# Half-rank sums behind gate blocks, whole transposes of keys and betas, and a score eviction split over two engines

## The chip, the core and the metric

The program runs on one core of a Trainium2 chip. The core has five engines that each take their instructions in a fixed order, written into the program when it is built: TensorE (PE in the profile, with its weight loads as PEld), VectorE (DVE), ScalarE (ACT), GpSimd (POOL) and SyncE (SP). Engines wait for each other by semaphores; an instruction that waits holds up everything behind it on its engine. DMAs are issued from the queues of SP, ACT and POOL. The metric is the device time of one execution in microseconds, the median of several runs.

## The reference

One block of a streaming encoder over 512 frames of width 1024, all in float32. What matters here is the RWKV-7 branch with 8 heads of 64:

```python
proj = h @ w_in + b_in                      # 4864 columns, 38 blocks of 128
r, k, v, pw, pa, pg = split(p + (token_shift(p) - p) * mu)
decay, a, g = ...                           # from pw, pa, pg by small matrices
kk = normalise(k * k_k); k = k * (1.0 + (a - 1.0) * k_a)
# per frame: S = S diag(w) + (S a) b^T + v k^T ; y = S r, with a = -kk, b = kk * a
y = group_norm(rwkv7_recurrence(r, decay, k, v, -kk, kk * a)) * lnx_g + lnx_b
bonus = sum(r * k * r_k, per head) * v
y_a = ((y + bonus) * g) @ w_branch_a
...
merged = sigmoid(gate_a) * y_a + sigmoid(gate_b) * y_b   # gates: 16 of the 38 blocks
x = x + merged @ w_mix_out                  # then cross-attention and a ConvFFN
```

## The kernel before

Feature channels lie on the 128 partitions and the 512 frames along the free axis. Every large product is made of three fp32r matmuls on splits into a high and a low part (`mm3`, L159 to L163). Weights stream in units of 128x1024: SP loads a raw unit (L102, four buffers), ACT casts the high part (L114), DVE subtracts for the low part (L115). One unit feeds one of the 38 blocks of the input projection, `inproj` (L516), 24 matmuls of 128x512 each. The order of the blocks is `IN_ORDER`: 14 RWKV blocks, then 16 gate blocks (22 to 37), then the 8 blocks of the other branch. Below, "block 20" is the block that uses `win_h20`.

Work on the heads runs in pairs, j = 0 to 3. `prep` and `prep2` make the scaled sequences: `AK` (alphas and receptances) and `KBt` (betas and keys, interleaved by chunk of 64 frames; the two heads of a pair are offset by one column block, which is why it has 2·NC+1 of them). `scores` multiplies them chunk by chunk on PE (L605, 128 matmuls) and DVE evicts each of the four groups of a pair with a mask in two instructions of 64x512 (`BZ` at L609, `AK` at L610). `bonus` then takes r·k·r_k (L586), sums it per head with a matrix of ones in two matmuls (`bo`, L156 and L157, after a split by ACT at L154 and DVE at L155), multiplies by v (L589), adds a bias (L590) and stores to `dBo` (L591), to be loaded again by the group norm much later.

The 64 small triangular systems (8 chunks by 8 heads) of the recurrence are solved next. `scores` sends the alpha parts to DRAM (`dM`, L612), SP gathers them transposed into `Nm` (L654, two DMAs), and DVE runs 31 dependent steps on `Zt` (`zz`, L660 and L661; `Zt` is set by L655 first). `Zt` returns through `dZt` and `dZ` to `ZA` (L665 to L677); PE completes the inverses with 32x32 matmuls (`zh` L687, `zo` L695). A sequential loop over 8 chunks follows (L753 to L804). For each chunk it needs rows of values (`rows_v`, L734) and of keys and betas (`rows_kb`): eight transposes from 64 partitions (L746) into two PSUM tiles and two ACT copies of 128x256 (L747). All the while, blocks of the input projection fill PE. POOL issues DMAs that sum later weights in DRAM; each waits for a chosen matmul.

A scheduler orders each engine's instructions by program order and priority when the program is built. The solve, the DMAs of the solve and the chunk loop have high priority; the first three gate blocks (`NEARLY`) are written before pair 3, the others after the chunk loop, where they fill.

Of the kernel before, what the change touches and what calls it, by code (L numbers as in the profile page):

```python
# [53 lines left out]
def hybrid_block_kernel(ctx: ExitStack, tc: tile.TileContext, xT_d, mT_d, pv_d, cst_d, win_d, wk_d, wv_d,  # L54
# [15 lines left out]
    def mm_ps(name):  # L70
        return pmm.tile([P, T], F32, tag="mm", name=name)
# [435 lines left out]
    for i in range(2):  # L507
        with tc.issue_after(wdma[-1].ins):
            nc.sync.dma_start(lraw[i], lup_d[i])
    uin = Units(win_d, "win")  # L510


    NSUM = {12: 1, 13: 1, 4: 1, 5: 1, 0: 1, 1: 1, 8: 1, 9: 1, 6: 2, 7: 2, 2: 2, 3: 2, 10: 2, 11: 2,
            22: 2, 23: 1, 27: 1, 28: 1, 29: 1, 15: 4, 16: 4, 17: 4, 18: 4, 19: 4, 20: 3, 21: 2}

    def inproj(i):  # L516
        ps = mm_ps(f"in_ps{i}")
        dense(ps, uin, lambda kb: (h2[:, 0, kb, :], h2[:, 1, kb, :]), KB, NSUM.get(i, 0))
        return ps
# [41 lines left out]
    def prep2(j, pk, pr, at, Pi, Pp):  # L561
# [13 lines left out]
        V.tensor_tensor(kk, kk, at, ALU.mult)  # L575
        V.tensor_tensor(KBt[:, j, 1::2, :], c3(kk), c3(Pi), ALU.mult)
        S.activation(at, at, AF.Identity, scale=par("k_a", j), bias=oka[:, j:j + 1])
        V.tensor_tensor(pk, pk, at, ALU.mult)
        V.tensor_tensor(KBt[0:HD, j, 2::2, :], c3(pk)[0:HD], c3(Pi)[0:HD], ALU.mult)
        V.tensor_tensor(KBt[HD:P, j, 0:2 * NC:2, :], c3(pk)[HD:P], c3(Pi)[HD:P], ALU.mult)  # L580
        for e in range(2):
            hs = half[e]
            V.tensor_tensor(AK[hs, e, jc, HD:P], c3(pr)[hs], Pp[hs, :, 1:], ALU.mult)

    def bonus(j, pk, pr):
        V.scalar_tensor_tensor(pr, pr, par("r_k", j), pk, ALU.mult, ALU.mult)  # L586
        ps = rw_ps(f"bo{j}")
        sum_exact(ps, bonesr, pr, tp, "xb", f"bo{j}")
        V.tensor_tensor(pr, ps, vT[:, j, :], ALU.mult)  # L589
        S.activation(pr, pr, AF.Identity, bias=par("lnx_b", j))  # L590
        nc.scalar.dma_start(dBo[j], pr)  # L591

    def kb_cols(j, e, c):
        return KBt[half[e], j, 2 * c + 1 - e:2 * c + 3 - e, :].rearrange("p a t -> p (a t)")

    def scores(j):
        for e in range(2):
            hs, oh = half[e], half[1 - e]  # L600
            for cg in range(2):
                ps = rw_ps(f"sc{j}_{e}_{cg}")
                i0 = j * NC + cg * 4
                for i in range(4):
                    PE.matmul(ps[:, i * P:(i + 1) * P], kb_cols(j, e, cg * 4 + i), AK[hs, e, i0 + i, :],  # L605
                              start=True, stop=True)
                p3 = ps.rearrange("p (c t) -> p c t", t=P)
                m3 = scmask.unsqueeze(1).to_broadcast([P, 4, P])
                V.tensor_tensor(BZ[hs, i0:i0 + 4, :], p3[hs], m3[hs], ALU.mult)  # L609
                V.tensor_tensor(AK[oh, e, i0:i0 + 4, :], p3[oh], m3[oh], ALU.mult)  # L610
# [10 lines left out]
    for jp in range(2):  # L621
# [10 lines left out]
        for j in js:  # L632
            if j == 3:
                for i in IN_REST[:NEARLY]:
                    gate_block(i - 22)
            at, L, Pp = prep(j)
            prep2(j, pks[j], prs[j], at, L, Pp)
            scores(j)
            bonus(j, pks[j], prs[j])

    pp_ctx.close()
    pq_ctx = ExitStack()
    pq = pq_ctx.enter_context(tc.tile_pool(name="pq", bufs=1, reuse_waits="tile"))
    YB = pq.tile([P, 4, T], F32, name="YB")

# [95 lines left out]
    def rows_kb(c):  # L741
        KBr = ch.tile([P, 2, NPAIR, HD], F32, tag="KBr", name=f"KBr{c}", bufs=2)
        for e in range(2):
            ps = ch_ps(f"kbr{c}_{e}", ("kv", "s")[e])
            for j in range(NPAIR):
                PE.transpose(ps[:, j * HD:(j + 1) * HD], kb_cols(j, e, c), ident[half[e], half[e]])  # L746
            S.copy(KBr[:, e], j3(ps[:, 0:256]))  # L747
        return KBr
# [4 lines left out]
    def chunk(c, UV, KBr, SP):  # L753
# [664 lines left out]
```

## Time and profile before

| | us |
|---|---|
| median of 3 runs | 912.09 (909.4, 912.09, 913.08) |
| the profiled execution, its own time | 909.73 |
| its span in the trace | 908.0 |
| TensorE busy | 890.5 |
| VectorE busy | 687.4 |
| ScalarE busy | 510.4 |
| GpSimd busy | 129.3 |

The profile comes from one execution. A row of its timeline has the start in us from the span's start, the length, the engine, the line, the operation, output and inputs, and in brackets how long the engine sat idle before it and what ended that. A PE matmul's record begins when it enters and ends when its result is out, so records overlap: the time that a matmul takes from PE is the distance from its start to the next one's start. The granted TensorE clock was 0.998 of full speed over the run.

### The profile page before, as it was taken

What the parts mean: (1) busy time and instruction counts of PE and PEld (TensorE: products, weight loads), DVE (VectorE), ACT (ScalarE), POOL (GpSimd) and SP (SyncE); (2) the same over time, 40 slices, a digit from 0 to 9 for tenths busy, and PEclk for the clock granted to TensorE, in tenths of its full rate; (3) what the DMA queues carried; (4) which work ended last, traced back from release to release, by engine and by line L of the source; (5) the groups of instructions that cost most, each with busy time, mean ns of one, the idle gap of its engine ahead of it and who ended that gap; (6) DMA issues with size and microseconds to landing.
All of it is one profiled execution on the core that took longest, in us unless ns stands there. A gap on an engine that the chain in (4) does not pass through costs nothing. (4 is left out here: it accounts for less than half of the span.)

```text
span 908.0 us, 15914 instructions
## 1 busy us (share of the span) xinstructions
PE 890.5 (98%) x6218; PEld 776.1 (85%) x6218; DVE 687.4 (76%) x1096; ACT 510.4 (56%) x779; POOL 129.3 (14%) x159
## 2 busy tenths in 40 slices
PE   7999999999999999999999999999999999999996
PEld 6988877788877777887887778999999999999996
DVE  7884598776957585776565568788998888999674
ACT  6674675542236675234454446765665556767663
POOL 0102222010011212001112211111111111201100
PEclk9999999999999999999999999999999999999999
DMA  8878899667499749858788868898989998998963
GB/s 276 277 263 230 186 237 208 179 165 206 139 205 246 167 106 194 258 180 223 210 243 190 177 152 185 240 273 247 280 249 290 258 316 251 248 277 222 269 197 93
DMA packets 102411, 200.07 MB, mean 220 GB/s; under 512 B 25344, under 2 KB 36736, under 8 KB 102272
## 3 DMA queue, kind: packets, MB, share of 16 engines
q1 hardware_dynamic: 69504, 119.75, 41.0%
q0 software_dynamic: 25504, 67.38, 36.8%
q10 hardware_dynamic: 7328, 11.92, 3.9%
q8 instruction: 49, 0.80, 0.3%
q14 instruction: 26, 0.21, 0.1%
HBM read 187.75 MB, written 77.59 MB: 292 GB/s over the span
## 5 line engine op out<-in xcount | busy, mean ns | idle before, releaser
L126 ACT CAST wfi_h<-wfi_r 128x1024 fp32r<-128x1024 f32 x77 | 81.0, 1052 | 76.8 <-PE fx_ps L161 21.1
L160 PE MATMUL in_ps<-hT,win_h 128*128 128x512 f32 x304 | 121.9, 402 | 0.8 <-DVE pr L525 0.7
L162 PE MATMUL in_ps<-hT,win_l 128*128 128x512 f32 x304 | 120.8, 398 | 0.0
L161 PE MATMUL in_ps<-hT,win_h 128*128 128x512 f32 x304 | 120.6, 398 | 0.0
L127 DVE TENSOR_TENSOR wfi_l<-wfi_r,wfi_h 128x1024 fp32r<-128x1024 f32 x77 | 94.0, 1221 | 23.5 <-ACT wfi_h L126 23.3
L425 POOL DMA_DIRECT2D dS<-in_wfi x66 | 66.5, 1044 | 267.0 <-PE in_ps L160 132.4
L114 ACT CAST win_h<-win_r 128x1024 fp32r<-128x1024 f32 x38 | 39.8, 1048 | 71.9 <-PE in_ps L161 70.9
L115 DVE TENSOR_TENSOR win_l<-win_r,win_h 128x1024 fp32r<-128x1024 f32 x38 | 46.4, 1221 | 32.6 <-ACT win_h L114 32.5
L160 PEld LDWEIGHTS in_ps<-hT,win_h 128*128 128x128 f32 x304 | 57.0, 187 | 15.6 <-DVE pr L525 1.1
L161 PEld LDWEIGHTS in_ps<-hT,win_h 128*128 128x128 f32 x304 | 57.0, 188 | 14.0 <-issue 0.7
L162 PEld LDWEIGHTS in_ps<-hT,win_l 128*128 128x128 f32 x304 | 57.0, 187 | 13.9 <-issue 0.2
L461 POOL DMA_DIRECT2D dOs<-in_wfo x54 | 39.9, 804 | 186.0 <-PE fx_ps L160 50.9
L1245 DVE TENSOR_TENSOR wfo_l<-wfo_r,wfo_h 128x1024 fp32r<-128x1024 f32 (+1 forms) x39 | 47.2, 1210 | 13.6 <-ACT wfo_h L1244 13.5
L1244 ACT CAST wfo_h<-wfo_r 128x1024 fp32r<-128x1024 f32 (+1 forms) x39 | 40.4, 1038 | 28.2 <-PE oyz_ps L161 9.8
L161 PE MATMUL fx_ps<-hr,wfi_h 128*128 128x256 f32 x176 | 49.7, 282 | 0.0
L162 PE MATMUL fx_ps<-hr,wfi_l 128*128 128x256 f32 x176 | 49.7, 282 | 0.0
L160 PE MATMUL ox_ps<-go,wfo_h 128*128 128x256 f32 x176 | 49.6, 282 | 0.1
L160 PE MATMUL fyz_ps<-hq,wfi_h 128*128 128x256 f32 x176 | 49.3, 280 | 0.4 <-ACT p L1173 0.4
L160 PE MATMUL fx_ps<-hq,wfi_h 128*128 128x256 f32 x176 | 49.5, 281 | 0.0
L160 PE MATMUL fx_ps<-hr,wfi_h 128*128 128x256 f32 x176 | 49.4, 281 | 0.0
L162 PE MATMUL ox_ps<-go,wfo_l 128*128 128x256 f32 x176 | 49.3, 280 | 0.0
L161 PE MATMUL ox_ps<-go,wfo_h 128*128 128x256 f32 x176 | 49.3, 280 | 0.0
(418 smaller groups left out, 2727.8 us busy)
## 6 DMA issues: line engine op xcount, KB each, us to landing
dS<-in_wfi POOLq DMA_DIRECT2D x66, 512.0 KB, 8.4
wfi_r<-dS SPq DMA_DIRECT2D x44, 512.0 KB, 6.9
win_r<-in_win SPq DMA_DIRECT2D x38, 512.0 KB, 5.0
wfi_r<-in_wfi SPq DMA_DIRECT2D x33, 512.0 KB, 5.6
dS<-dS POOLq DMA_DIRECT2D x22, 512.0 KB, 5.7
dOs<-in_wfo POOLq DMA_DIRECT2D x12, 512.0 KB, 7.8
wv_r<-in_wv SPq DMA_DIRECT2D x8, 512.0 KB, 4.9
dG<-gs ACTq DMA_DIRECT2D x16, 256.0 KB, 2.6
```

The lines of the kernel that those rows point to most:

```text
L114: S.copy(hi[:, o:o + n], raw[:, o:o + n])
L115: V.tensor_tensor(lo[:, o:o + n], raw[:, o:o + n], hi[:, o:o + n].bitcast(F32), ALU.subtract)
L126: S.copy(hi, raw)
L127: V.tensor_tensor(lo, raw, hi.bitcast(F32), ALU.subtract)
L160: first = PE.matmul(ps, lh, rh, start=start, stop=False, **kw)
L161: PE.matmul(ps, lh, rl, start=False, stop=False, **kw)
L162: PE.matmul(ps, ll, rh, start=False, stop=stop, **kw)
L425: return lambda: nc.gpsimd.dma_start(s(out), src, **kw)
L461: yield lambda k=k, w=w, src=src: nc.gpsimd.dma_start(dO[n, m][:, k * P:(k + w) * P], src, **kw)
L1244: S.copy(hi[:, :n], raw[:, :n])
L1245: V.tensor_tensor(lo[:, :n], raw[:, :n], hi[:, :n].bitcast(F32), ALU.subtract)
```

## The change

Four things are changed.

First, `bonus` is cut in two. After `scores(j)`, `bonus_terms(j)` makes only the product r·k·r_k and stores it to `dBo` (128x512, from ACT's queue). After the last pair, all four are loaded back (`bt`, from ACT's queue, two buffers), split by ACT (`bhi`, which lives where `YB` comes later) and DVE (`blo`). Five gate blocks (25 to 29, up to `NMID`) are now written ahead of the solve, and the two `bo` matmuls of a pair, the product with v (`bs`), the bias and the second store to `dBo` are placed behind such a block's last matmul in program order.

Second, `KBt` loses its extra column. `prep2` writes it with four DVE instructions on 64 partitions instead of one on 128 and two on 64.

Third, `rows_kb` uses four transposes from all 128 partitions into one PSUM tile and one ACT copy of 128x512, in place of eight transposes, two tiles and two copies.

Fourth, in `scores` DVE multiplies only the right half of the `BZ` part by the mask (64x4x64); the left, alpha half is copied by ACT without a mask. Most of that half is later overwritten with the completed inverses; the one 32x32 corner per chunk and head that stays has to be zero, and POOL clears it with two memsets.

```diff
-        V.tensor_tensor(KBt[:, j, 1::2, :], c3(kk), c3(Pi), ALU.mult)
-        V.tensor_tensor(KBt[0:HD, j, 2::2, :], c3(pk)[0:HD], c3(Pi)[0:HD], ALU.mult)
-        V.tensor_tensor(KBt[HD:P, j, 0:2 * NC:2, :], c3(pk)[HD:P], c3(Pi)[HD:P], ALU.mult)
+        for e in range(2):
+            hs = half[e]
+            V.tensor_tensor(KBt[hs, j, e::2, :], c3(kk)[hs], c3(Pi)[hs], ALU.mult)
+            V.tensor_tensor(KBt[hs, j, 1 - e::2, :], c3(pk)[hs], c3(Pi)[hs], ALU.mult)
...
-    def bonus(j, pk, pr):
+    def bonus_terms(j, pk, pr):
         V.scalar_tensor_tensor(pr, pr, par("r_k", j), pk, ALU.mult, ALU.mult)
+        nc.scalar.dma_start(dBo[j], pr)
+    def bonus(j, hi, lo, after):
         ps = rw_ps(f"bo{j}")
-        sum_exact(ps, bonesr, pr, tp, "xb", f"bo{j}")
-        V.tensor_tensor(pr, ps, vT[:, j, :], ALU.mult)
-        S.activation(pr, pr, AF.Identity, bias=par("lnx_b", j))
-        nc.scalar.dma_start(dBo[j], pr)
+        with tc.issue_after(after.ins):
+            PE.matmul(ps, bonesr, hi, start=True, stop=False)
+            PE.matmul(ps, bonesr, lo, start=False, stop=True)
+        bt = tp.tile([P, T], F32, tag="xb", name=f"bs{j}", bufs=2)
+        V.tensor_tensor(bt, ps, vT[:, j, :], ALU.mult)
+        S.activation(bt, bt, AF.Identity, bias=par("lnx_b", j))
+        nc.scalar.dma_start(dBo[j], bt)
...
-                V.tensor_tensor(BZ[hs, i0:i0 + 4, :], p3[hs], m3[hs], ALU.mult)
                 V.tensor_tensor(AK[oh, e, i0:i0 + 4, :], p3[oh], m3[oh], ALU.mult)
+                V.tensor_tensor(BZ[hs, i0:i0 + 4, HD:P], p3[hs, :, HD:P], m3[hs, :, HD:P], ALU.mult)
+                S.copy(BZ[hs, i0:i0 + 4, 0:HD], p3[hs, :, 0:HD])
...
+    bhi = pq.tile([P, NPAIR, T], F32R, tag="YB", name="bhi")
+    blo = [tp.tile([P, T], F32R, tag=("ga", "gx")[j % 2], name=f"blo{j}", bufs=2) for j in range(NPAIR)]
+    for j in range(NPAIR):
+        bt = tp.tile([P, T], F32, tag="xb", name=f"bt{j}", bufs=2)
+        nc.scalar.dma_start(bt, dBo[j])
+        S.copy(bhi[:, j, :], bt)
+        V.tensor_tensor(blo[j], bt, bhi[:, j, :].bitcast(F32), ALU.subtract)
+    for k, i in enumerate(IN_REST[NEARLY:NMID]):
+        gate_block(i - 22)
+        if k:
+            bonus(k - 1, bhi[:, k - 1, :], blo[k - 1], last_in)
...
+    for e in range(2):
+        nc.gpsimd.memset(BZ[HD * e + 32:HD * e + 64, :, 0:32], 0.0)
...
-        KBr = ch.tile([P, 2, NPAIR, HD], F32, tag="KBr", name=f"KBr{c}", bufs=2)
-        for e in range(2):
-            ps = ch_ps(f"kbr{c}_{e}", ("kv", "s")[e])
-            for j in range(NPAIR):
-                PE.transpose(ps[:, j * HD:(j + 1) * HD], kb_cols(j, e, c), ident[half[e], half[e]])
-            S.copy(KBr[:, e], j3(ps[:, 0:256]))
+        KBr = ch.tile([P, NPAIR, P], F32, tag="KBr", name=f"KBr{c}", bufs=2)
+        ps = ch_ps(f"kbr{c}", "kv")
+        for j in range(NPAIR):
+            PE.transpose(ps[:, j * P:(j + 1) * P], kb_cols(j, slice(0, P), c), ident)
+        S.copy(KBr, ps.rearrange("p (j i) -> p j i", i=P))
...
-    for i in IN_REST[NEARLY:]:
+    for i in IN_REST[NMID:]:
```

The order of the engines moves at three places. The first is ACT after the last pair's scores. In the kernel before, ACT casts `bo3_h`, adds the bias for pair 3 and stores it there, between the casts of weights (`win_h`) and the sigmoids of the gate blocks (`gs`):

```order
L114 CAST win_h22_2808<-win_r22_2806 128x1024
L154 CAST bo3_h_1728<-pr3_1354 128x512
L237 ACTIVATE gs5_2732<-in_ps27_2700,pv_75 128x512
L619 DMA dG_712<-gs5_2732 128x512
L590 ACTIVATE pr3_1354<-pr3_1354,pv_75 128x512
L591 DMA dBo_713<-pr3_1354 128x512
L114 CAST win_h23_2842<-win_r23_2840 128x1024
L237 ACTIVATE gs6_2767<-in_ps28_2735,pv_75 128x512
L619 DMA dG_712<-gs6_2767 128x512
```

In the changed kernel ACT copies the alpha halves out of the scores' PSUM tiles (`sc3`), stores the product of pair 3 (`pr3`), and then casts the four reloaded products; the loads of the third and fourth stand behind the casts of the first two:

```order
L626 COPY BZ_743<-sc3_1_1_1710 64x4x64
L593 DMA dBo_713<-pr3_1346 128x512
L115 CAST win_h22_2795<-win_r22_2793 128x1024
L239 ACTIVATE gs5_1854<-in_ps27_1822,pv_75 128x512
L635 DMA dG_712<-gs5_1854 128x512
L666 CAST bhi_1725<-bt0_1730 128x512
L666 CAST bhi_1725<-bt1_1734 128x512
L665 DMA bt2_1738<-dBo_713 128x512
L665 DMA bt3_1742<-dBo_713 128x512
L115 CAST win_h23_2829<-win_r23_2827 128x1024
L666 CAST bhi_1725<-bt2_1738 128x512
L239 ACTIVATE gs6_1896<-in_ps28_1864,pv_75 128x512
```

So the cast of `bt2` stands between the weight cast for block 23 and the sigmoid of gate block 28, and waits there for a load that is issued three rows earlier.

The second is DVE between the last score eviction and the first step of the inner solve. Before, it ran so (`sc3` are the scores of pair 3, `win_l` the low parts of weights):

```order
L610 TENSOR_TENSOR AK_746<-sc3_1_1_1718,cst_76 64x512
L586 SCALAR_TENSOR_TENSOR pr3_1354<-pr3_1354,pv_75,pk3_1278 128x512
L717 SCALAR_TENSOR_TENSOR cst_76<-cst_76 128x128
L115 TENSOR_TENSOR win_l22_2809<-win_r22_2806,win_h22_2808 128x1024
L155 TENSOR_TENSOR bo3_l_1729<-pr3_1354,bo3_h_1728 128x512
L589 TENSOR_TENSOR pr3_1354<-bo3_1727,vT_745 128x512
L115 TENSOR_TENSOR win_l23_2843<-win_r23_2840,win_h23_2842 128x1024
L655 MEMSET Zt_1746 128x1024
L656 MEMSET Zt_1746 128x32
L115 TENSOR_TENSOR win_l24_2877<-win_r24_2874,win_h24_2876 128x1024
L660 TENSOR_TENSOR zz_1748<-Zt_1746,Nm_1745 128x1
```

In the changed kernel, behind the product of pair 3 (L592) and the small product on `cst`:

```order
L116 TENSOR_TENSOR win_l22_2796<-win_r22_2793,win_h22_2795 128x1024
L683 MEMSET Zt_1953 128x1024
L667 TENSOR_TENSOR blo0_1726<-bt0_1730,bhi_1725 128x512
L667 TENSOR_TENSOR blo1_1727<-bt1_1734,bhi_1725 128x512
L684 MEMSET Zt_1953 128x32
L116 TENSOR_TENSOR win_l23_2830<-win_r23_2827,win_h23_2829 128x1024
L667 TENSOR_TENSOR blo2_1728<-bt2_1738,bhi_1725 128x512
L667 TENSOR_TENSOR blo3_1729<-bt3_1742,bhi_1725 128x512
L602 TENSOR_TENSOR bs0_1818<-bo0_1815,vT_745 128x512
L602 TENSOR_TENSOR bs1_1860<-bo1_1857,vT_745 128x512
L688 TENSOR_TENSOR zz_1955<-Zt_1953,Nm_1952 128x1
```

The first step on `Nm` now has four subtractions for `blo` and the products `bs0` and `bs1` ahead of it, and all of these stand behind the memset of `Zt`. The products `bs2` and `bs3` come later, between steps of the solve.

The third is PE where the completed solve is first used (`zh`, beside block 32 before, `ga` and `gx` being two products of the other branch). Before:

```order
L161 MATMUL in_ps16_3190<-hT2_1_90,win_h32_3193 128x512
L162 MATMUL in_ps16_3190<-hT2_0_89,win_l32_3194 128x512
L160 MATMUL in_ps16_3190<-hT2_0_89,win_h32_3193 128x512
L161 MATMUL in_ps16_3190<-hT2_1_90,win_h32_3193 128x512
L687 MATMUL zh0_0_1828<-ZA_1823,BZ_743 32x32 x16
L162 MATMUL in_ps16_3190<-hT2_0_89,win_l32_3194 128x512
```

In the changed kernel, beside block 31:

```order
L163 MATMUL in_ps15_3111<-hT2_0_89,win_l31_3115 128x512
L161 MATMUL in_ps15_3111<-hT2_0_89,win_h31_3114 128x512
L717 MATMUL zh0_0_2037<-ZA_2030,BZ_743 32x32 x16
L883 MATMUL ga0_3101<-xb0_3095,rg_751 128x512
L162 MATMUL in_ps15_3111<-hT2_1_90,win_h31_3114 128x512
```

PE meets `zh` thirteen projection matmuls and one pair of `ga` and `gx` earlier in its order than before. The `bo` matmuls of the four pairs, which stood among the blocks of pairs 0 to 3 and block 20, now stand in blocks 20 and 21: `bo0` and `bo1` from the ninth matmul of block 20 on, `bo2` behind the seventh of block 21 and `bo3` behind its last. The chunk loop's first `vr` also comes earlier, in block 33 rather than at its end, so that 44 projection matmuls lie within the loop where 39 did.

More of the change, by code (lines that the diff above doesn't have):

```diff
@@ L33 @@
 NEARLY = 3
+NMID = 8
 IN_ORDER = IN_RWKV + IN_REST
@@ L180, in dense @@
                 sum_behind(ins)
+        return ins
     class Split:
@@ L480, in hybrid_block_kernel @@
     BZ = pa.tile([P, NPAIR * NC, P], F32, tag="AR", name="BZ")
-    KBt = big.tile([P, NPAIR, 2 * NC + 1, HD], F32, tag="x16", name="KBt")
+    KBt = big.tile([P, NPAIR, 2 * NC, HD], F32, tag="x16", name="KBt")
     vT = pa.tile([P, NPAIR, T], F32, name="vT")
@@ L510, in hybrid_block_kernel @@
     uin = Units(win_d, "win")
+    last_in = None
     NSUM = {12: 1, 13: 1, 4: 1, 5: 1, 0: 1, 1: 1, 8: 1, 9: 1, 6: 2, 7: 2, 2: 2, 3: 2, 10: 2, 11: 2,
@@ L516, in inproj @@
     def inproj(i):
+        nonlocal last_in
         ps = mm_ps(f"in_ps{i}")
-        dense(ps, uin, lambda kb: (h2[:, 0, kb, :], h2[:, 1, kb, :]), KB, NSUM.get(i, 0))
+        last_in = dense(ps, uin, lambda kb: (h2[:, 0, kb, :], h2[:, 1, kb, :]), KB, NSUM.get(i, 0))
         return ps
@@ L583, in prep2, with kb_cols @@
             V.tensor_tensor(AK[hs, e, jc, HD:P], c3(pr)[hs], Pp[hs, :, 1:], ALU.mult)
-    def bonus(j, pk, pr):
+    def bonus_terms(j, pk, pr):
         V.scalar_tensor_tensor(pr, pr, par("r_k", j), pk, ALU.mult, ALU.mult)
+        nc.scalar.dma_start(dBo[j], pr)
+    def bonus(j, hi, lo, after):
         ps = rw_ps(f"bo{j}")
-        sum_exact(ps, bonesr, pr, tp, "xb", f"bo{j}")
-        V.tensor_tensor(pr, ps, vT[:, j, :], ALU.mult)
-        S.activation(pr, pr, AF.Identity, bias=par("lnx_b", j))
-        nc.scalar.dma_start(dBo[j], pr)
-    def kb_cols(j, e, c):
-        return KBt[half[e], j, 2 * c + 1 - e:2 * c + 3 - e, :].rearrange("p a t -> p (a t)")
+        with tc.issue_after(after.ins):
[5 more added lines that the diff above has]
+        nc.scalar.dma_start(dBo[j], bt)
+    def kb_cols(j, hs, c):
+        return KBt[hs, j, 2 * c:2 * c + 2, :].rearrange("p a t -> p (a t)")
     def scores(j):
@@ L604, in scores @@
                 for i in range(4):
-                    PE.matmul(ps[:, i * P:(i + 1) * P], kb_cols(j, e, cg * 4 + i), AK[hs, e, i0 + i, :],
+                    PE.matmul(ps[:, i * P:(i + 1) * P], kb_cols(j, hs, cg * 4 + i), AK[hs, e, i0 + i, :],
                               start=True, stop=True)
@@ L638, in hybrid_block_kernel @@
             scores(j)
-            bonus(j, pks[j], prs[j])
+            bonus_terms(j, pks[j], prs[j])
     pp_ctx.close()
@@ L643, in hybrid_block_kernel @@
     pq = pq_ctx.enter_context(tc.tile_pool(name="pq", bufs=1, reuse_waits="tile"))
-    YB = pq.tile([P, 4, T], F32, name="YB")
+    bhi = pq.tile([P, NPAIR, T], F32R, tag="YB", name="bhi")
[9 more added lines that the diff above has]
+            bonus(k - 1, bhi[:, k - 1, :], blo[k - 1], last_in)
+    YB = pq.tile([P, 4, T], F32, tag="YB", name="YB")
     with tc.tile_pool(name="pz", bufs=1, reuse_waits="tile") as pz:
@@ L780, in chunk @@
                 for e in range(2):
-                    PE.matmul(pss[half[e], j * HD:(j + 1) * HD], KBr[:, e, j, :], UV[:, e, j, :],
+                    PE.matmul(pss[half[e], j * HD:(j + 1) * HD], KBr[:, j, half[e]], UV[:, e, j, :],
                               start=True, stop=True)
```

## The prediction

> **What bounds the kernel now.** I read the page first. The second row gives the busy time of each engine, the third is TensorE's busy share in 40 equal slices of the span, the last begins the chain of waits.
>
> ```profile
> span 908.0 us, 15914 instructions
> PE 890.5 (98%) x6218; PEld 776.1 (85%) x6218; DVE 687.4 (76%) x1096; ACT 510.4 (56%) x779; POOL 129.3 (14%) x159
> PE   7999999999999999999999999999999999999996
> PE 28%; DVE 1%; ACT 0%; DVEq 0%; issue 0%
> ```
>
> TensorE is the bound in every slice. Only two things count: work taken off it, and the time for which its next instruction waits. Records of matmuls overlap, so short waits hide in the busy share; they show as a longer distance between starts. From the timeline between 118 and 172 us, TensorE alone:
>
> ```profile
> 119.30 0.47 PE L156 MATMUL bo<-bo_h,bonesr 128*128 128x512 f32 x1 [0.55 <-DVE AK L610]
> 132.68 0.39 PE L162 MATMUL in_ps<-hT,win_l 128*128 128x512 f32 x1
> 133.74 0.50 PE L160 MATMUL in_ps<-hT,win_h 128*128 128x512 f32 x1 [0.67 <-DVE pr L525]
> 144.01 0.39 PE L548 MATMUL psa<-pwa,llo 128*128 128x512 f32 x1
> 144.75 0.49 PE L157 MATMUL bo<-bo_l,bonesr 128*128 128x512 f32 x1 [0.35 <-DVE bo_l L155]
> 145.41 0.50 PE L160 MATMUL in_ps<-hT,win_h 128*128 128x512 f32 x1 [0.17 <-DVE pk L525]
> 170.86 0.40 PE L160 MATMUL in_ps<-hT,win_h 128*128 128x512 f32 x1
> 171.49 0.50 PE L157 MATMUL bo<-bo_l,bonesr 128*128 128x512 f32 x1 [0.23 <-DVE bo_l L155]
> 265.20 0.39 PE L160 MATMUL in_ps<-hT,win_h 128*128 128x512 f32 x1
> 265.44 0.40 PE L161 MATMUL in_ps<-hT,win_h 128*128 128x512 f32 x1
> ```
>
> A projection matmul normally takes 0.234 us (265.20 to 265.44, and 24 of them a block). The waits above are 0.55 at 119.30; 0.74−0.23 = 0.51 and 0.66−0.23 = 0.43 around 144.75; 0.63−0.23 = 0.40 before 171.49: 1.9 us at `bo`. One more, 1.06−0.23 = 0.83 before 133.74, is VectorE being late with an eviction.
>
> **The change part by part: pairs 0 to 3.** All `bo` matmuls leave this stretch, and with them the 1.9 us. VectorE loses two operations and halves four per pair, and gains one. Its groups between 110 and 215 us (lines, shapes, count, busy time and mean in ns, idle time before):
>
> ```profile
> L609 DVE TENSOR_TENSOR BZ<-sc,cst 64x512 f32<-64x512 f32 x16 | 11.0, 686 | 0.3
> L576 DVE TENSOR_TENSOR KBt<-kk,L 128x512 f32<-128x512 f32 x4 | 2.7, 687 | 0.0
> L589 DVE TENSOR_TENSOR pr<-bo,vT 128x512 f32<-128x512 f32 x4 | 2.7, 683 | 1.2 <-PE bo L157 1.2
> L155 DVE TENSOR_TENSOR bo_l<-pr,bo_h 128x512 fp32r<-128x512 f32 x4 | 2.7, 678 | 0.0
> ```
>
> Per pair: −0.68 (`bo_l`), −0.68 (product with v), 4 × about −0.33 (half of 0.686; an estimate, as the instruction's fixed part isn't seen), +0.69 (a fourth `KBt` instruction; time goes by length, 64 or 128 partitions alike): −2.0 us. So part of the 0.83 goes too. Against that, each score tile is now read by two engines, and ACT's copy of the alpha half waits until VectorE is done with the tile; with `bo` gone, `ss` matmuls are next in line to wait. I take 2.3 us gained, between 1.0 (new waits of about 0.5 at two places, none of the 0.83) and 2.7 (1.9 and all 0.83). Six `bo` matmuls of pairs 0 to 2, 6 × 0.234 = 1.4 us, are also moved behind this stretch: the end of pair 3's scores comes 3.7 us earlier, but those 1.4 us are paid in blocks 20 and 21.
>
> **The reload.** The products go to DRAM and back, at the worst moment: SP issues the two gathers `Nm` then.
>
> ```profile
> 196.60 0.45 PE L156 MATMUL bo<-bo_h,bonesr 128*128 128x512 f32 x1
> 197.78 8.65 SPq L654 DMA_DIRECT2D Nm<-dM  x2
> DMA to landing us min/median/max: 13.4/13.7/13.9
> 199.97 0.33 ACTq L591 DMA_DIRECT2D dBo<-pr  x1
> DMA to landing us min/median/max: 6.7/6.7/6.7
> 206.98 0.91 DVE L655 MEMSET Zt<- 128x1024 f32 x1 [3.62 <-DMA dBo<-pr]
> 212.45 0.16 DVE L660 TENSOR_TENSOR zz<-Zt,Nm 128x1 f32<-128x1 f32 x1 [3.22 <-DMA Nm<-dM]
> dG<-gs ACTq DMA_DIRECT2D x16, 256.0 KB, 2.6
> ```
>
> The third row is the time from issue to landing of the two `Nm` gathers, the fifth that of the `dBo` store at 199.97 alone. This store of 256 KB took 6.7 us amid the gathers, and the memset of `Zt` waited 3.62 for it; the usual one takes 2.6 (last row, the median of sixteen `gs` stores). After the change: `pr3` is stored some 4 us before its product's old end, still outside the jam, since `Nm` needs two `dM` landings first. `Nm` is issued at 197.78 − 3.7 + 0.7 = 194.8 (the 0.7: one more `KBt` instruction and ACT's copy ahead of the last `dM`, less VectorE's shorter evictions). The loads of `bt2` and `bt3` follow the casts of `bt0` and `bt1` and their subtractions, which free the two buffers: about 196, inside the jam. At 6.7 to 7 us they land at 203; the cast (0.6) is done at 203.6. TensorE meets `bo2` at about 199.5: the old `bo_h` of pair 3 is met at 196.60 (row above) and 24 matmuls on is 202.2, plus 1.0 for the four matmuls of `bo0` and `bo1` now in between, less 3.7. **It waits 4 us in all** there and at `bo0`; with loads of 2.6 us nothing, with 13.4 some 10.
>
> By the Trainium skill ("DMA: Bandwidth & Descriptors", Anatomy of one DMA: 2.0 us and bytes/436e3 per us) a 256 KB transfer is worth 2.6 us. The usual stores agree, the one in the jam (6.7) does not; by the page `bo2` would hardly wait, which is the first rival below.
>
> **The solve.** This decides what is left of the gain.
>
> ```profile
> 258.53 2.75 SPq L676 DMA_DIRECT2D ZA<-dZt  x2
> DMA to landing us min/median/max: 7.0/7.0/7.0
> 263.78 1.12 PE L855 MATMUL gx<-xb,rg 128*128 128x512 f32 x2
> 264.97 0.39 PE L162 MATMUL in_ps<-hT,win_l 128*128 128x512 f32 x1
> 266.45 1.19 PE L687 MATMUL zh<-ZA,BZ 32*32 32x32 f32 x32
> ```
>
> The first `ZA` load, issued at 258.53, takes 7.0 us (second row, for it alone) and lands at 265.55; TensorE meets `zh` at 266.45. So there was 0.9 us of slack. In the changed order `zh` stands 13 matmuls and a `ga`, `gx` pair earlier: 13 × 0.234 + 2 × 0.96 (263.78 to 264.97 is one `gx`, which shows as two records, and a projection matmul: 1.19 − 0.23) = 5.0 us. TensorE would be there at 266.45 − 5.0 − 2.3 + 4 = 263.1. The solve comes 3.7 earlier by the scores, +0.7, and +1.4 for `bs2` and `bs3` (2 × 0.68), which VectorE does between its steps: 1.6 earlier, between 0.3 and 2.7 by the bounds above (1.4 + 1.0 − 2.1, and 1.4 + 2.7 − 1.4 where the 0.7 is nothing). `zh` then starts at 265.55 − 1.6 = 264.0, with 5.0 us more work behind it than before: 264.0 + 5.0 − 266.45 = **+2.6 us at this point**, between +1.4 and +3.8. A shorter wait at `bo2` would not help; it would be waited at `zh`.
>
> **The transposes.** Rows from the chunk loop, and whole 128x128 transposes of the attention:
>
> ```profile
> 293.66 0.46 PE L746 MATMUL kbr<-cst,KBt 64*128 64x64 f32 x4
> 294.05 0.50 PE L160 MATMUL in_ps<-hT,win_h 128*128 128x512 f32 x1
> 294.39 0.40 PE L161 MATMUL in_ps<-hT,win_h 128*128 128x512 f32 x1
> 474.88 0.44 PE L1028 MATMUL prT_ps<-cst,ex 128*128 128x128 f32 x2
> 475.08 0.48 PE L160 MATMUL q_ps<-hx,wq_h 128*128 128x512 f32 x1
> L747 ACT COPY KBr<-kbr 128x256 f32<-128x256 f32 x16 | 5.9, 372 | 1.7 <-PE kbr L746 1.4
> ```
>
> Four half transposes take 0.39 us to the next start, and the matmul behind them 0.34 instead of 0.23. Two whole ones take 0.20: 0.10 each, four 0.40. Per chunk 0.78 − 0.40 = 0.38, times eight 3.0 us, and six changes between tile shapes fewer at 0.11: 0.6. **−3.6 us**, between −2.5 (0.46 for four, no change saved) and −5.5 (both quads between projections, two changes each). The loop has projection matmuls to fill in, so TensorE's time counts, not the loop's latency. ACT's eight copies of 128x512 (0.6, as its casts of that shape) replace 16 of 0.372: a microsecond less on an engine that is 56% busy, nothing on the path.
>
> In the Trainium skill ("TensorE: Matmul & The Clock Gate", Part 4) a transpose of 128x128 is measured at about 275 ns. Taken as the time from start to start, 32 would be 8.8 us in place of 6.2, and the change would end at +2.6 + 2.6 = +5.2, 917.3: slower. By the rows a pair's records last 0.44, but the next matmul starts 0.20 after the pair, so I leave this a chance of 0.01.
>
> **The memsets and the rest.** POOL's two memsets of the corners stand among its sums, which wait for TensorE anyway. Four stores and four loads of 256 KB more are 2 MB, 1% of the 200 that the run moves. Both: nothing, up to 0.5. SP issues `win_r26` behind `Nm` now rather than ahead; four raw buffers cover it.
>
> **Sum** against the profiled 909.73: +2.6 − 3.6 = −1.0, so 908.7. The profiled run lies 2.4 under the median of 912.09, whose runs spread over 3.7; the same difference on the median gives **911.1**. The forecast's own range is 908 to 913.5: the bounds of the solve and of the transposes, +1.4 − 5.5 and +3.8 − 2.5.
>
> **The rivals.**
> - *The whole gain* (chance 0.25). The loads come in the usual 2.6 us because `Nm`'s packets leave room, and the solve keeps step with TensorE, its gathers too landing sooner, so that `zh` finds `ZA`. For it: most of VectorE's work ahead of the solve goes. Against: the memset row. −2.3 − 3.6 = −5.9: 906.2, down to 904.3 with the upper bound of the transposes.
> - *The reload stalls the solve* (0.13), slower. `blo2` and `blo3` stand ahead of the first step `zz` on VectorE, and `bhi2` ahead of the sigmoid and the weight casts on ACT. If the loads take as long as `Nm` itself (13.4) or `pr3`'s store also falls into the jam and the memset of `Zt` waits for it first, the loads land at 209.5 to 212. TensorE loses 10 to 12 at `bo2` and comes to `zh` at 269 to 271, where the solve, started at 213 to 215, is no earlier: −2.3 + 10.4 − 3.6 = +4.5, up to +6: 916.6 to 918. It decides from a landing at about 210. For it: the row of 6.7. Against: that same store, issued 2 us into the jam, landed over 4 us ahead of `Nm` (206.7 against 197.78 + 13.4).
> - *The change frees nothing* (0.14). ACT's alpha copies wait for VectorE in any case, new waits at `ss` and `sc` take the 1.9 us back, so the solve comes only 0.3 earlier and costs +3.8, which eats the 3.6 of the transposes. 0: 912.1. For it: one matmul in the pairs is already held by an eviction (133.74).
>
> **How the numbers follow.** The forecast has 0.47, and 0.01 stands beside the transposes. Half a per cent (4.6 us, about what a measurement of this kernel can tell from no change) puts the bounds at 907.5 and 916.6: faster 0.25, same 0.61, slower 0.14. The range of 8 in 10 takes in the first rival and stops short of the second: 905 to 915.5.
>
> **What would show it.** Right: no wait at `bo` or at 133.7 in the pairs; four `kbr` in about 0.4 us, 32 in all; `bo2` late by a load (a wait on `bhi` L666, itself on a DMA of `bt`); a wait at the first `zh` of a few tenths to a microsecond. Wrong: `bt2` landing in under 3 us after issue, or over 12; a first `zz` step later than 212; whole transposes 0.17 apart; new waits of TensorE on `sc` evictions in the pairs.

## The result, and the profile after

| | before | after |
|---|---|---|
| median of 12 runs each, us | 910.09 (909.31 to 913.08) | 915.77 (912.47 to 921.41) |
| the profiled execution | 909.73 | 915.84 |
| its span | 908.0 | 914.1 |
| granted TensorE clock over it | 0.998 | 0.996 |

The changed kernel takes 1.006 times the time of before (95% interval 1.0044 to 1.0076). The forecast was 911.1 with a range of 905.0 to 915.5. The forecast stood on 912.09, the median of three runs of before; on the 910.09 of twelve runs the same −1.0 gives 909.1, so the miss is larger than 915.77 against 911.1 looks. On the profiled executions, against which the sum was made, −1.0 was predicted and +6.1 came: 7.1 us are to be explained.

The page of after, with the rows that were shown of before (span, busy times, TensorE's slices, the start of the chain):

```profile
span 914.1 us, 15911 instructions
PE 890.6 (97%) x6186; PEld 774.9 (85%) x6186; DVE 685.6 (75%) x1100; ACT 515.7 (56%) x787; POOL 131.1 (14%) x161
PE   7999999989999999998999999999999999999996
PE 84%; DMA 7%; DVE 6%; ACT 2%; issue 1%; DVEq 0%; SPq 0%; ACTq 0%
```

TensorE is as busy as before (890.6 against 890.5), but two slices of its row have an 8, the ninth and the nineteenth, and VectorE and DMAs now have a share of the chain. The first of the two slices holds the reload. From the timeline of after, TensorE, ACT and ACT's queue (start, length, instruction, and in brackets the idle time before it):

```profile
196.80 0.92 ACTq L665 DMA_DIRECT2D bt<-dBo  x2
DMA to landing us min/median/max: 6.2/6.3/6.5
199.96 0.39 PE L161 MATMUL in_ps<-hT,win_h 128*128 128x512 f32 x1
203.01 0.62 ACT L666 CAST bhi<-bt 128x512 fp32r<-128x512 f32 x1 [3.44 <-DMA bt<-dBo]
203.69 0.50 PE L599 MATMUL bo<-bhi,bonesr 128*128 128x512 f32 x1 [3.34 <-ACT bhi L666]
204.40 0.63 PE L163 MATMUL in_ps<-hT,win_l 128*128 128x512 f32 x1
204.83 0.63 PE L161 MATMUL in_ps<-hT,win_h 128*128 128x512 f32 x1
```

TensorE stands from 199.96 to 203.69 at `bo2`: 3.73 − 0.23 = 3.5 us. What follows was not predicted: the matmuls behind the wait start 0.43 apart (204.40 to 204.83) instead of 0.23. The granted clock of TensorE tells why. In each row below stand a stretch, its length, the busy time of PE, PEld, DVE, ACT and POOL with the number of their instructions, then the granted clock, the DMAs' share and their GB/s:

```profile
203.00:204.00 1.00, 0.32 (x1) 0.30 (x2) 0.34 (x1) 0.98 (x2) 0.00 (x0) 1.00 1.18 222
204.00:207.50 3.50, 3.50 (x10) 2.73 (x9) 2.34 (x4) 2.02 (x4) 0.00 (x0) 0.51 1.23 221
207.50:209.00 1.50, 1.50 (x8) 1.22 (x7) 0.56 (x4) 0.09 (x1) 0.00 (x0) 1.00 0.97 310
```

For 3.5 us the clock is 0.51, and 0.49 × 3.5 = 1.7 us are lost by it. Below, a stretch at such a clock is called **half speed**; what is lost by it is the length of the stretch times what its granted clock lacks of 1. Block 21 took 11.67 us in place of 5.6: the wait 3.5, four `bo` matmuls 0.94, and 1.6 of half speed.

The nineteenth slice (411 to 434 us) begins with the mix, the end of the branch, where merged values have met their gates. Waits in a stretch are given as waiting instruction, releaser, then total, count and longest. TensorE from 355 to 440 us and VectorE from 355 to 410 us, the landing times of the eight `gb` loads, and POOL's last sums ahead of the mix, after:

```profile
PE mix_ps L161 <- ACT mg L963: 1.7, 1, 1.7
PE mix_ps L162 <- DVE mg L964: 0.7, 1, 0.7
PE yb_ps L161 <- DVE mB L947: 0.5, 1, 0.5
PE yb_ps L162 <- DVE yb L940: 0.4, 1, 0.4
DVE mB L947 <- DMA gb<-dG: 7.3, 5, 3.2
DVE gta L961 <- DMA gta<-dG: 4.7, 4, 2.9
DMA to landing us min/median/max: 2.8/6.1/8.8
369.29 1.85 POOL L427 DMA_DIRECT2D dS<-in_wfi  x2 [5.44 <-DMA dS<-dS]
```

The same views before had:

```profile
PE yb_ps L161 <- DVE yb L910: 0.4, 1, 0.4
DVE mB L917 <- DMA gb<-dG: 4.3, 4, 2.4
DVE gta L931 <- DMA gta<-dG: 1.3, 2, 1.1
DMA to landing us min/median/max: 2.9/3.9/9.2
362.14 1.85 POOL L425 DMA_DIRECT2D dS<-in_wfi  x2 [5.42 <-DMA dS<-dS]
```

The loads of the gates land later, and VectorE and then TensorE wait for them. Two of POOL's weight sums are now issued at 369.29, 7 us later than before, amid the `gb` loads, which are issued from 356.8 to 382.5 (before: from 353.7 to 378.2).

To see where time is won and lost, the starts of the same matmuls are compared with those in before (after minus before, us, read from the timelines):

| first matmul of | predicted | after | bonus later | bt2 early | zh held |
|---|---|---|---|---|---|
| block 20 | −3.7 | −3.1 | −3.1 | −2.5 | −2.9 |
| block 22 | +1.7 | +3.5 | −3.2 | −1.9 | −3.0 |
| block 31, just ahead of `zh` | +1.7 | +3.5 | −1.8 | −1.9 | −1.6 |
| `yb_ps`, past the chunk loop | −1.0 | +1.3 | −0.3 | +4.2 | −4.6 |
| `q`, past the mix | −1.0 | +5.3 | +0.2 | +4.5 | −4.0 |
| end of the span | −1.0 | +6.1 | +1.4 | +6.8 | −4.0 |

The predicted +1.7 is −3.7 + 4 + 6 × 0.234; past `zh` +2.6 was predicted, and +3.7 came (265.14 − 266.45 + 5.0, `zh` standing 5.0 us of work earlier). The last three columns are three of the experiments below (one profile each).

### The profile page after: what moved, and what is told of

Same layout as the page of the kernel before. It is cut to its first block, busy times and chain, and to the rows that moved or that the text cites. A ratio compares the mean times of both kernels' runs of the same rounds, so it can differ in the third digit from the quotient of the medians.

```text
span 914.1 us, 15911 instructions
## 1 busy us (share of the span) xinstructions
PE 890.6 (97%) x6186; PEld 774.9 (85%) x6186; DVE 685.6 (75%) x1100; ACT 515.7 (56%) x787; POOL 131.1 (14%) x161
## 4 chain that ended last, share of the span: by engine, by line
PE 84%; DMA 7%; DVE 6%; ACT 2%; issue 1%; DVEq 0%; SPq 0%; ACTq 0%
PE in_ps L161 7%; PE in_ps L162 7%; PE in_ps L163 7%; PE fx_ps L161 5%; PE fx_ps L163 5%; PE fx_ps L162 5%; PE fyz_ps L161 3%; PE fyz_ps L163 3%; PE fyz_ps L162 3%; DMA gta<-dG 2%; PE co_ps L161 2%; PE q_ps L162 2%; PE co_ps L163 2%; PE q_ps L161 2%; PE q_ps L163 2%; DMA gb<-dG 2%
## 5 line engine op out<-in xcount | busy, mean ns | idle before, releaser
L1275 DVE TENSOR_TENSOR wfo_l<-wfo_r,wfo_h 128x1024 fp32r<-128x1024 f32 (+1 forms) x39 | 47.1, 1208 | 14.6 <-ACT wfo_h L1274 14.4
```

Source lines behind the costliest of these rows:

```text
L1275: V.tensor_tensor(lo[:, :n], raw[:, :n], hi[:, :n].bitcast(F32), ALU.subtract)
```

## The experiments

The theory: the loss is the wait at `bo2` with its half speed, and then the late gate loads. The rivals: the other operations themselves (split eviction, transposes) cost time; or the solve, no earlier than before, takes back whatever is gained elsewhere. The experiments ran in four groups, each with runs of before beside it, whose medians were 910.18, 911.16, 910.39 and 910.71.

### Which part carries the loss

**Part one undone**: the changed kernel with `bonus` as it was before; the keys' layout, the transposes and the split eviction stay.

```diff
-    def bonus_terms(j, pk, pr):
+    def bonus(j, pk, pr):
         V.scalar_tensor_tensor(pr, pr, par("r_k", j), pk, ALU.mult, ALU.mult)
+        ps = rw_ps(f"bo{j}")
+        sum_exact(ps, bonesr, pr, tp, "xb", f"bo{j}")
...
```

> The change with its first part undone: the sums over r, k and r_k stand behind each pair's scores as in the kernel before, with no store and reload; whole transposes, key and beta layout and the split score eviction stay. If the reload makes the whole loss (a wait of 3.5 us at bo2, 1.7 us of half-speed matmuls behind it, 4 us of waits at the yb and mix products from sums that come later), this run has none of them and keeps the transposes' 2.3 to 3.6 us: 906 to 908, under the kernel before. If the score eviction or the transposes cost time too, it is 910 or more.

917.15 us, ratio 1.0076 (1.0058 to 1.0094): slower, where a gain was expected. Its waits of TensorE between 100 and 250 us:

```profile
PE sc L610 <- DVE KBt L585: 5.2, 1, 5.2
PE bo L157 <- ACT BZ L616: 0.7, 2, 0.4
```

The scheduler has put pair 1's score matmuls ahead of block 12, and they wait 5.2 us for a `KBt` that isn't written yet, with half speed behind: the granted clock is 0.57 from 139 to 151 us, and 5.2 us are lost by it. At the pairs' end it is 10.3 us behind before, which these two make up. So the reason is the order that came out, not the operations' own cost, and this run says nothing on what these are worth.

**Part one alone** on the kernel before:

> The kernel before with the first part of the change alone (store, reload and the bo matmuls at gate blocks 20 and 21). If the reload makes the loss: a wait of 3 to 4 us at bo2 with slow matmuls behind it, and 915 to 919, as without the transposes' gain. If the loss comes from the other parts: 909 to 911.

915.72, ratio 1.0057 (1.0037 to 1.0077): as slow as the whole change. `bo2`'s wait is there, 2.3 us, but without half speed behind it (the granted clock is 1.00 from 100 to 890 us). In its timeline:

```profile
201.78 0.50 PE L598 MATMUL bo<-bhi,bonesr 128*128 128x512 f32 x1 [2.29 <-ACT bhi L663]
202.12 0.40 PE L161 MATMUL in_ps<-hT,win_h 128*128 128x512 f32 x1
202.35 0.39 PE L162 MATMUL in_ps<-hT,win_h 128*128 128x512 f32 x1
```

At block 22 it is 0.4 us ahead of before, at the end 3.7 behind; some 2 us of that come in the attention, where a matmul waits for ScalarE's exponentials, which was not examined further. The profiled execution took 913.4, 2.3 under the median of this kernel, so a part of its loss is in no trace.

**The bonus later**: the changed kernel, with the four `bo` pairs at the ends of the blocks 21 to 24 instead of in 20 and 21.

```diff
-NMID = 8
+NMID = 11
...
-        if k:
-            bonus(k - 1, bhi[:, k - 1, :], blo[k - 1], last_in)
+        if k > 3:
+            bonus(k - 4, bhi[:, k - 4, :], blo[k - 4], last_in)
```

> The change with the bo matmuls three gate blocks later (behind blocks 21 to 24, one pair each), by when all four reloads have landed. If the wait at bo2 and what hangs on it is the cause: no wait at bo, no half-speed matmuls, 5.2 us less or more: 905 to 910. If the late sums of POOL in the chunk loop make a loss of their own that does not hang on this wait, the waits at yb and mix (4 us) stay and it is 910 to 912.

911.61, ratio 1.0009 (0.9995 to 1.0023): 4.2 us under the changed kernel, level with before. Nothing waits at `bo` any more, but `zh` does, as the prediction said it would, and here too half speed follows (a granted clock of 0.72 from 266 to 272 us, 1.7 us lost):

```profile
265.27 1.19 PE L717 MATMUL zh<-ZA,BZ 32*32 32x32 f32 x32 [2.15 <-DMA ZA<-dZt]
267.84 0.63 PE L161 MATMUL in_ps<-hT,win_h 128*128 128x512 f32 x1
268.27 0.63 PE L162 MATMUL in_ps<-hT,win_h 128*128 128x512 f32 x1
```

TensorE is there at 263.1 (265.27 − 2.15), 3.3 us sooner than in before: 1.8 by what has been gained, the rest because fewer matmuls stand ahead of `zh`. The solve isn't sooner: `ZA` lands at 265.23, in before at 265.57. In the tail VectorE waits 1.6 us for `gta`, where the changed kernel waits 4.7. TensorE loses 0.6 us between `yb_ps` and `q` instead of 4.0: block 34 starts only 5.5 us later than in before, and POOL's last two sums ahead of the mix are issued at 358.5. So the later bonus takes away not the wait at `bo2` alone.

**The sums earlier**: the changed kernel with POOL's sums spread over more blocks, so that none is issued amid the gates' loads. `NSUM` and the forecast number the blocks by their columns: 30 to 37 are the gate blocks from block 22 on, 17 to 21 are blocks 33 to 37.

```diff
-             22: 2, 23: 1, 27: 1, 28: 1, 29: 1, 15: 4, 16: 4, 17: 4, 18: 4, 19: 4, 20: 3, 21: 2}
+             22: 2, 23: 1, 27: 1, 28: 1, 29: 1, 30: 1, 31: 1, 32: 1, 33: 1, 34: 1, 35: 1, 36: 1, 37: 1,
+             15: 4, 16: 4, 17: 3, 18: 2, 19: 2, 20: 1, 21: 1}
```

> The change with eight of POOL's sums paced by gate blocks 30 to 37 rather than by blocks 17 to 21; all else in the same order. If the waits at yb and mix (4 us against the kernel before) come from sums whose traffic meets the loads of the gates there: these waits fall under 1.5 us and the time to 911 to 913, the wait at bo2 staying. If they come from the order of VectorE's or ScalarE's work: 915 to 916.

The mechanism came, the gain didn't: 917.62, ratio 1.009 (1.0065 to 1.0116). From `yb_ps` to `q` it loses 0.3 us where the changed kernel loses 4.0. The last sum ahead of the mix is issued 7 us ahead of `yb_ps`, the `gb` loads take 2.8 us in the median instead of 6.1, and the waits of `mB` for them are gone; of `gta` 1.4 are left:

```profile
DVE gta L962 <- DMA gta<-dG: 1.4, 1, 1.4
PE bo L600 <- ACT bhi L667: 3.3, 1, 3.3
PE zo L726 <- issue: 1.9, 1, 1.9
```

But the new order has a wait of 1.9 at `zo`, again with half speed behind, so that it comes to `yb_ps` 3.1 us later than the changed kernel.

### The other parts alone, and the wait at bo2

**The keys' layout and whole transposes alone** on the kernel before:

> The kernel before with the new layout of keys and betas and the whole transposes alone (parts two and three). In the change and in the run with late bo matmuls TensorE gained 2.3 us between block 22 and the yb products; if that is the transposes', this run is 907.5 to 908.5 with the gain between 285 and 345 us. By the prediction's working (3.6) it is 906 to 907. If the gain of those runs came from the order of the chunk loop, 910.

912.73, ratio 1.0018 (1.0000 to 1.0036). Its two largest waits of TensorE between 100 and 300 us, four whole transposes in the chunk loop, and their group (busy us, mean ns, idle before):

```profile
PE in_ps L160 <- DVE pk L525: 2.0, 2, 1.8
PE bo L156 <- ACT bo_h L154: 1.9, 1, 1.9
296.22 0.66 PE L747 MATMUL kbr<-cst,KBt 128*128 128x128 f32 x4
296.63 0.48 PE L162 MATMUL in_ps<-hT,win_l 128*128 128x512 f32 x1
L747 PE MATMUL kbr<-cst,KBt 128*128 128x128 f32 x32 | 6.2, 292 | 0.0
```

The two waits, and half speed behind the first (a granted clock of 0.76 from 128 to 135 us; 1.00 around the second), put it 4.3 us behind; the chunk loop gives 3.0 back (+4.3 at block 31, +1.3 at `yb`). Four whole transposes take 296.63 − 296.22 = 0.41 us.

**The split eviction and the memsets alone** on the kernel before:

> The kernel before with the split score eviction and the two memsets alone (part four). If the lighter VectorE helps: the pairs end about 1 us earlier and the waits at bo shrink, 908.5 to 910. If ACT's alpha copies, which wait for VectorE, only add a link to the chain and change the order on TensorE: new waits of TensorE in pairs 0 to 3, 911 or more.

929.93, ratio 1.0197 (1.0173 to 1.0221), with two long waits, both with half speed behind (a granted clock of 0.61 from 137 to 150 and of 0.66 from 277 to 287 us, 5.1 and 3.4 us lost):

```profile
PE in_ps L160 <- DVE pr L525: 4.9, 1, 4.9
PE zh L690 <- DMA ZA<-dZt: 4.1, 1, 4.1
```

The two waits and what is lost behind them make 17.5 of the 20.8 us by which the profiled execution is longer than that of before. On the medians the first part alone loses 5.5 us to before, the transposes 1.6, the split eviction 18.8, and the whole change 5.7: the parts don't add up, since each edit gives the scheduler another order with waits of its own.

**bt2 loaded early**: the third product gets a buffer of its own, so its load need not follow the cast of the first.

```diff
-        bt = tp.tile([P, T], F32, tag="xb", name=f"bt{j}", bufs=2)
+        bt = tp.tile([P, T], F32, tag="st" if j == 2 else "xb", name=f"bt{j}", bufs=2)
```

> The change with the third reload in a buffer of its own (one of the gates' buffers), so that it is issued before the Nm gathers rather than among them; bo0 to bo2 stand at blocks 19 and 20 then and bo3 at the end of block 21. If the two-buffer chain of loads inside the gathers makes the wait at bo2: no wait there, no half-speed matmuls, 4 to 6 us less than the change, 909 to 912, the solve then ending last at zh (a wait of 1 to 2 us). If the loads are slow wherever they stand: bo1 or bo2 waits and 914 or more.

915.78, ratio 1.0052 (1.0034 to 1.0070): no gain. The wait at `bo2` is gone (block 22 at −1.9 instead of +3.5), and the time is waited at the solve:

```profile
PE zh L717 <- DMA ZA<-dZt: 3.8, 1, 3.8
```

Behind it the granted clock is 0.66 from 265 to 275 and 0.76 from 285 to 292 us: another 5.1 us, more than the wait itself.

**The wait filled**: the changed kernel with 14 matmuls, whose result is thrown away, issued ahead of `bo2`, so that TensorE isn't idle while it waits.

```diff
+            for _ in range(fill):
+                PE.matmul(ps, bonesr, bhi[:, 0, :], start=True, stop=True)
             PE.matmul(ps, bonesr, hi, start=True, stop=False)
```

> The change with 14 matmuls of 128x512 whose result is thrown away (3.3 us of work) ahead of bo2, which stands three matmuls earlier for it. If TensorE's half speed behind bo2 comes from its idle time: at most 1 us of idle at bo2, then distances of 0.234 us from start to start and no record of 0.63 us. If it comes from the gathers or the load on the chip at that time: 0.43 us distances at 204 to 207 us as in the change.

One execution, 918.8. The place itself answers:

```profile
202.41 0.49 PE L604 MATMUL bo<-bhi,bonesr 128*128 128x512 f32 x1 [0.88 <-ACT bhi L671]
203.94 0.40 PE L161 MATMUL in_ps<-hT,win_h 128*128 128x512 f32 x1
204.17 0.40 PE L162 MATMUL in_ps<-hT,win_h 128*128 128x512 f32 x1
```

0.88 of idle time is left, and the matmuls behind keep 0.23 (the granted clock is 1.00 from 100 to 900 us): block 22 starts at +1.9, where the changed kernel has +3.5. So with the gathers and the load on the chip as they were, half speed went when the idle time went. The end, +9.1, is worse, through other waits in the tail (2.1 at `yb_ps`, 1.5 at the mix, 1.3 at `zo`).

### With the wait gone, the solve

**zh held**: on the kernel with the later bonus, the rest of the gate blocks that were written behind the chunk loop and three blocks of the other branch (`px_gates`) are written ahead of `zh`, which is issued behind the tenth matmul of a fixed later block. This gives the solve time without TensorE standing.

```diff
+            if kb == 3:
+                marks.append(ins)
...
+    for i in IN_REST[NMID:16]:
+        gate_block(i - 22)
+    two = [px_gates(0), px_gates(1)]
+    for p in two:
+        px_scan(*p)
+    px_2 = px_gates(2)
+    zh_after = marks[-1]
...
+                    with tc.issue_after(zh_after.ins):
+                        PE.matmul(psh[e][k, i * 32:(i + 1) * 32], BZ[r, i0 + i, 32:64], ZA[r, e, i0 + i, :],
```

> The run with late bo matmuls (e3), with the first zh matmuls held behind the tenth matmul of block 32 rather than the first; later work keeps its places. If the 2.2 us wait for ZA at zh and the half-speed matmuls behind it are what is left of the loss: the wait falls under 0.5 us, no half-speed matmuls there, and 2 to 3.5 us less than e3: 908 to 909.5, under the kernel before by 1 to 3. If the chunk loop or the tail is what is left: 911 to 912 as in e3.

Median 908.28, ratio 0.9990 (0.9969 to 1.0012): the fastest, but not told apart from before. Its profiled execution took 905.72, and there TensorE has no wait over 0.4 us from 100 us on:

```profile
265.36 1.19 PE L760 MATMUL zh<-ZA,BZ 32*32 32x32 f32 x32
PE mix_ps L162 <- ACT mg L977: 0.4, 1, 0.4
```

That is 4.0 under the profiled execution of before, where the first rival, the whole gain, had 5.9. But seven of its twelve executions took 905.7 to 908.9, four 910.0 to 911.4 and one 918.0, at clocks of 0.997 or more, 0.993 to 0.995, and 0.988: the fewer cycles granted, the longer.

**The product with v behind the solve's steps**: on the kernel with the later bonus, ACT evicts `bo`, and VectorE's four products `bs` wait for the end of the inner solve.

```diff
-        V.tensor_tensor(bt, ps, vT[:, j, :], ALU.mult)
+        S.copy(bt, ps)
+        return bt
...
+        with tc.issue_after(zn.ins):
+            V.tensor_tensor(bt, bt, vT[:, j, :], ALU.mult)
```

> The run with late bo matmuls, with ScalarE evicting bo and VectorE's product with v put behind the inner solve, so that VectorE does nothing but weights between its steps. If these products stretch the solve: its steps take 39.4 us as in the kernel before, not 42.0, and ZA lands 2 to 3 us sooner, near 262.5; the order on TensorE meets zh at block 31 in this kernel, so a wait of 2 to 4 us there may stay.

One execution, 927.07. The 31 steps take 39.4 us, as before, instead of 42.0, and the first `ZA` lands at 263.21 instead of 265.23: the products did cost the steps 2.6 us, and the landing of `ZA` 2.0. But the order has new waits elsewhere, 4.7 at `yb_ps` the largest:

```profile
PE yb_ps L161 <- DVE mB L956: 4.7, 2, 3.1
PE zh L723 <- DMA ZA<-dZt: 3.7, 1, 3.7
```

**zh held longer**: as "zh held", issued behind the 16th and the 22nd matmul instead of the tenth (`kb == 5`, `kb == 7`), to see if the spread of its executions comes from a `ZA` that lands just in time.

> As e10, with the first zh matmuls held behind the sixteenth matmul of block 32 (1.4 us more room for ZA). In e10's executions the granted clock went from 0.998 (906 to 908) to 0.988 (918). If ZA's landing, which varies, makes this spread: it narrows, the slow executions become fewer, and the median is 907 to 908, clear of the kernel before. If the spread comes from elsewhere it stays and the median is 908 to 909.

> As e10, with the first zh matmuls held behind the twenty-second matmul of block 32 (2.8 us more room). The same forecasts as for the sixteenth; if holding zh back costs more than the wait that it saves, since all of the chunk loop hangs on it, 909 or more.

911.69 (ratio 0.9996, 0.9973 to 1.0019) and 911.72 (0.9997, 0.9976 to 1.0019): level with before, over the 907 to 909 that were forecast, and for the 22nd within its "909 or more". The spread stayed (906.35 to 915.70, and one execution of 920.31; 906.41 to 914.59). In the profile of the 22nd the wait has gone to the other `ZA` gathers, a step on:

```profile
PE zo L768 <- DMA ZA<-dZ: 2.1, 1, 2.1
```

So more room for the first gather alone doesn't narrow the spread. What makes it stays open.

## Why the prediction was wrong, point by point

**Pairs 0 to 3: right.** Block 20 starts 3.1 us earlier, 3.7 were predicted. The `bo` waits are gone, and of the 0.83 before 133.74 at most 0.2 is left; TensorE's waits between 110 and 200 us, ahead of the reload, are now:

```profile
PE ss L158 <- DVE q L527: 0.2, 1, 0.2
PE in_ps L161 <- DVE pr L529: 0.2, 1, 0.2
PE in_ps L161 <- DVE pk L529: 0.2, 1, 0.2
```

The halved eviction takes 0.42 us, so 0.26 are saved and not the estimated 0.33:

```profile
L625 DVE TENSOR_TENSOR BZ<-sc,cst 64x256 f32<-64x256 f32 x16 | 6.8, 422 | 0.2
```

**The reload: right in its mechanism and length.** The loads were issued at 196.80 (predicted 196), landed at 203.0 (203), the cast ended at 203.63 (203.6), and the wait was 3.5 (4).

**One failed step** is the price of that wait: "**It waits 4 us in all**", counted as 4 us, and carried on to `zh` as "+2.6 us at this point". A wait of this length was followed by 1.6 us lost at half speed, and filling it took them away. At block 22 TensorE was 3.5 us behind before instead of 1.7: 0.6 from the pairs and 1.6 of half speed, less 0.5 for the shorter wait. Past `zh` it was 3.7 behind instead of 2.6. The bound of +3.8 covered this, but for another reason.

**The solve: only in part.** The prediction had `ZA` land 1.6 us earlier and TensorE wait for it. It landed 5.1 earlier, at 260.49: the first step came at 208.34 instead of 212.45, the steps took 40.5 instead of 39.4, and the load 4.8 in place of 7.0. So in the changed kernel TensorE came to `zh` last, at 265.14. But "A shorter wait at `bo2` would not help; it would be waited at `zh`" holds where it was tried: with `bt2` early (3.8 at `zh`), and for a part with the bonus later (2.15). In these the scores end about 3 us earlier and `ZA` lands at 266.7 and 265.2, before at 265.57. The two products on VectorE between the steps were priced at 1.4, and the steps took 1.1 longer; with all four there they take 42.0.

**The transposes: right in kind, the size off.** Four take 0.41, 0.40 were predicted. Over the loop, without waits in the way, 3.0 us were gained (transposes alone, and "zh held": −1.6 to −4.6), in the changed kernel 2.4 from `zh` on (+3.7 to +1.3); 3.6 were predicted. So 0.6 of the 1.2 that lack is the size of the term. The other 0.6 belongs to the order of the changed kernel, where the scheduler splits some groups of four; that this is the reason isn't shown:

```profile
309.44 0.33 PE L776 MATMUL kbr<-cst,KBt 128*128 128x128 f32 x1
310.31 0.55 PE L776 MATMUL kbr<-cst,KBt 128*128 128x128 f32 x3
```

**The failed step that weighs most** is a term that the sum doesn't have. Behind the chunk loop it counts nothing, and of POOL's sums the prediction says no more than that they "wait for TensorE anyway" ("nothing, up to 0.5", for the memsets among them). The chunk loop now stands about a block earlier among the projection blocks, so blocks 34 and 35 start later (block 34 by 27.9 us, block 35 by 14.6), and POOL's sums, which wait for matmuls of these blocks, are issued later with them. They meet the gates' loads, of which the `gb` take 6.1 us in the median instead of 3.9, and TensorE loses 4.0 us between `yb_ps` and `q`. That earlier sums take this loss away is shown ("the sums earlier": 0.3); that the whole time falls by as much is not, since that order lost elsewhere. The other profiles mostly agree. POOL's last two sums ahead of the mix are issued 9.5 us behind the first `yb_ps` in the changed kernel, 8.1 with the wait filled and 8.7 with the product behind the solve, and 4.0, 4.9 and 6.8 us are lost there. In before and eight others they come at most 3.6 behind it, and at most 0.6 is lost. Two don't fit, with early sums and a loss all the same, whose cause stays open: the split eviction alone (2.6), and "zh held" at the 16th matmul in its execution of 920.31 (5.0).

Together: 7.1 = 1.1 at `zh` + 1.2 in the transposes + 4.0 in the tail + 0.8 in the FFN, of which 0.5 is one wait of TensorE for VectorE in its output (`ox_ps` for `wfo_l`); why that came was not examined. Against its own 912.09 the range went from −7.1 to +3.4: the first two terms leave the end at +1.3, well inside, and the tail carries it out. Of the rivals, "the reload stalls the solve" had the sign (+4.5 to +6) but not the reason: the loads landed at 203, long before 210. What the split eviction is worth by itself stays open, as its order never came without waits of its own. "Zh held" shows that the whole change can be had without these waits in an execution; a version that beats before on its median was not found.

## What to carry to other kernels

On a kernel that is bound by its matmuls and has an order fixed when it is built, price a wait of 2 to 4 us at TensorE with what can come behind it, here 1.7 us more of half speed at `bo2` and up to 5.2 elsewhere, and look whether something can fill it. When a stage moves, go through every queue whose work is paced by the matmuls that move with it, and ask which loads that traffic now meets. Don't infer what a part is worth from a kernel with that part alone, unless the waits of its order have been read: of the four kernels here with some parts of the change and not all, three had waits of 2 to 5 us that the whole change hasn't.

## What the runs showed of the hardware

Half speed came after idle times of TensorE of 3.34 us (after), 2.15 (bonus later) and 3.75 (bt2 early), and also after 1.83 (transposes alone, at 129.4 us), 1.9 (sums earlier, at `zo`) and 1.6 (product behind the solve, at `zo`). It didn't come after 2.29 (part one alone), 1.89 (transposes alone, at 147.9), 1.71 (after, at the mix) nor after 0.88 (wait filled). In the changed kernel it lasted for some 3.4 us, with 0.43 instead of 0.23 from matmul to matmul; by the clock lost, it lasted as long with the bonus later, and three times as long, in two stretches, with `bt2` early. The Trainium skill ("TensorE: Matmul & The Clock Gate", Part 1) has the array at half its clock after an idle window of about 3.4 us and back at full speed after some 3.4 us of work, the window running freely. The halving and its shortest duration agree with the rows. That less than 2 us were enough, where the page's rule of thumb warns of gaps over about 3.4, doesn't agree; that 2.29 were not would fit a window that runs freely, which no run here tests.

The loads of 256 KB that were issued beside the fine-grained `Nm` gathers (`bt2` and `bt3`) took 6.2 to 6.5 us in the changed kernel, as the one store of before had (6.7). `bt1`, issued at 176.9, took 2.7. With `bt2` and `bt3` issued ahead of the gathers they took 3.7 and 2.9. But `bt0`, at 173.6 and far from the gathers, took 4.5, so they aren't all that lengthens a load.
